# A transformer block on one core: the FFN's down products filled in two halves of columns, each group one product later

## The chip, the cores and the metric

The kernel runs on one core of a Trainium2 chip (trn2). The metric is the device time in microseconds of one execution; three runs of the kernel before give a median of 2186.89 us (2186.75 to 2187.51). The profile is of one more execution, recorded by the hardware profiler.

## What is computed

One decoder block on x of shape (1, 512, 2048) in float32: an RMS norm, one input projection that feeds two groups of attention heads, an output projection, then a SwiGLU FFN with 5632 hidden units, and a final RMS norm. The change touches the FFN alone, which the reference computes so (cut):

```python
hn2 = rmsnorm(h, norm2_g[l])
h = h + (jax.nn.silu(hn2 @ w_gate[l]) * (hn2 @ w_up[l])) @ w_down[l]
return rmsnorm(h, final_g)
```

`w_gate` and `w_up` are 2048 x 5632, `w_down` is 5632 x 2048.

## The kernel before

Everything is kept transposed: channels on the 128 partitions, the 512 tokens as columns. A float32 product is made of three matmuls on split operands (high and low parts in the type fp32r): high weights x high activations, high weights x low activations, low weights x high activations. `mm3` (line 164) and `mm` (line 1009) issue such a trio. Each matmul has a weight load of 128 x 128 ahead of it.

**Halves.** Weights stream in as tiles of 128 x 512, four blocks of 128 x 128. A `Job` (line 123) turns one such tile into a high part on ACT (`first`, line 136, written `wh`) and a low part on DVE (`second`, line 139, written `wl`). Five buffers each rotate. `next_half` (line 172) takes the next job for TensorE, makes sure that the splits run three halves ahead (line 175), and then runs the deferred work in `lag` that has come due; `later(n, f)` (line 183) defers `f` until the half that is n after the next one is about to be issued. In `wsplit` (line 119) the weights lie 32 floats into their buffer where a job has `even=True`, else 16 floats; the streamed operands `ah` and `al` lie 32 floats in. All jobs ahead of the FFN have `even=True`; in the FFN only the first half of P1 for f in (1, 2) or f % 8 == 5 has (line 795).

**Gate and up.** For each of 44 blocks f of 128 hidden units, gate and up are computed together by a scheme of seven products, P1 to P7, in place of eight, on two halves of 256 tokens and 1024 channels. Each product is two halves of 12 matmuls with 256 columns (`product`, line 997). The order for f > 0 is P1, P7, P4, P6, P5, P2, P3. DVE makes the weight sums that the scheme needs (`comb`, line 753) and the sums of products (`after`, line 1027). `finish` (line 1014) then makes silu(gate) x up, splits it, and writes it into block 12 + f % 4 of `ah` (ACT, line 1021) and `al` (DVE, line 1025). For f the chain from the last product P3 to the written `al` is deferred into the products of f + 1: it ends at the half after P7.

**Down.** After four blocks f the four blocks 12 to 15 hold 512 hidden units, and 16 down products (`down`, line 1063) add their share to the 16 blocks of `hs`, the result in SBUF. One down is one half: a tile of `w_down`, 4 blocks x 3 matmuls with 512 columns, into one full bank of PSUM. Two banks rotate in the first group of downs (ph 0), three later. The bank is added to `hs` by DVE (lines 1076 and 1077), due two halves on; in the first group DVE also scales `hs` first. The tiles come by DMA from SP into two buffers (`rawd`, `load_dn`, line 732): each is requested when the one two before it has been split. Gate/up weights come into `raw` (four buffers, `load_to`, line 102), through the same queue.

The downs of one group are set among the seven products of the next f with f % 4 == 0 (f = 4, 8, ..., 40: ten groups, 160 downs), in the list that lines 810 to 823 write out. The last 16 downs are made in the last stage (`last`, line 1103), in halves of 256 tokens, the first half of all 16 outputs ahead of the second, with weights held in tiles that the FFN has finished with.

Of the kernel before, what the change touches and what calls it, by code (L numbers as in the profile page):

```python
# [23 lines left out]
PH = 4  # L24
# [47 lines left out]
def block_kernel(ctx: ExitStack, tc: tile.TileContext, xt, wst, wdn, smalls, wg, w2c, bias, ident_in, out):  # L72
# [17 lines left out]
    ah = slot["h"][:, MH:MH + KB * S].rearrange("p (a b) -> p a b", b=S)  # L90
    al = slot["l"][:, ML:ML + KB * S].rearrange("p (a b) -> p a b", b=S)
# [72 lines left out]
    def mm3(o, wh, wl, mh, ml, start, stop):  # L164
        pe.matmul(o, wh, mh, start=start, stop=False)  # L165
        pe.matmul(o, wh, ml, start=False, stop=False)  # L166
        pe.matmul(o, wl, mh, start=False, stop=stop)  # L167
# [4 lines left out]
    def next_half():  # L172
        i = pos["half"]
        pos["half"] += 1
        split_to(i + (AHEAD[i] if i < len(AHEAD) else 3 if i < len(jobs) - KB - 1 else 4))
        if i < n_plain:
            load_to(i // 2 + LA)
        while lag and lag[0][0] <= i:
            lag.popleft()[1]()
        j = jobs[i]  # L180
        return j.h, j.l

    def later(n, f):
        i = len(lag)
        while i and lag[i - 1][0] > pos["half"] + n:
            i -= 1
        lag.insert(i, (pos["half"] + n, f))
# [464 lines left out]
    def proj_block(upto=None):  # L652
        return ps.tile([128, 512], F32, tag="proj", name="pp", bufs=2)
# [40 lines left out]
    for j in range(NH):  # L694
# [5 lines left out]
        p = proj_block()  # L700
# [8 lines left out]
        p = proj_block()  # L709
# [3 lines left out]
        p = proj_block()  # L713
# [5 lines left out]
        p = proj_block()  # L719
# [81 lines left out]
    def dn_job(p, nb):  # L801
        return Job(lambda: dn[p, nb], post=load_dn)
# [8 lines left out]
    for f in range(FB):  # L811
        qj = quad_jobs(f, ORDER if f else ORDER0)
        p = f // PH - 1
        nb = 0
        for i, name in enumerate(ORDER if f else ORDER0):
            sched.append(("q", f, name))
            jobs += qj[2 * i:2 * i + 2]
            if f and f % PH == 0 and i:
                for _ in range(3 if i < 5 else 4):
                    if nb < KB:  # L820
                        sched.append(("d", p, nb))
                        jobs.append(dn_job(p, nb))
                        nb += 1
# [6 lines left out]
    def out_unit(half, tag="proj"):  # L830
        p = ps.tile([128, 512], F32, tag=tag, name="pab", bufs=2)
        c = 8 - 8 * half
        run_unit([(p, ah[:, c + k, :], al[:, c + k, :], k == 0, k == 7) for k in range(8)])
        return p
# [54 lines left out]
    for nb in range(KB):  # L889
        while "hs" not in rest and (nb == 4 and not idle() or nb == 2 and (queue or cur["s"])):  # L890
            step()
        p = out_unit(1, ("proj", "sc", "t")[nb // 2 % 3])
# [13 lines left out]
    LO, HI = slice(0, 256), slice(256, 512)  # L906
# [72 lines left out]
    for i in range(KB):  # L979
        nb = PASS2[i]  # L980
        p = out_unit(0)
# [27 lines left out]
    def mm(o, wh, wl, mh, ml, start, stop):  # L1009
        pe.matmul(o, wh, mh, start=start, stop=False, skip_group_check=True)  # L1010
        pe.matmul(o, wh, ml, start=False, stop=False, skip_group_check=True)  # L1011
        pe.matmul(o, wl, mh, start=False, stop=stop, skip_group_check=True)  # L1012
# [50 lines left out]
    def down(ph, nb):  # L1063
        n = nb % (3 if ph else 2)
        if n not in dbanks:
            dbanks[n] = banks["P3"] if not n else (ps.tile([128, 512], F32, tag="t", name="pd", bufs=2) if n == 1 else
                                                ps.tile([128, 512], F32, tag="misc", name="pd"))
        p = dbanks[n]
        h, l = next_half()
        for i in range(PH):  # L1070
            mm3(p, h[:, 128 * i:128 * i + 128], l[:, 128 * i:128 * i + 128], ah[:, 12 + i, :], al[:, 12 + i, :],
                i == 0, i == PH - 1)

        def add():
            if not ph:
                dve.tensor_tensor(hs[:, nb, :], hs[:, nb, :], st["inv"], op=OP.mult)
            dve.tensor_tensor(hs[:, nb, :], hs[:, nb, :], p, op=OP.add)  # L1077

        later(1, add)

    for kind, a, b in sched:
        if kind == "d":
            down(a, b)
            continue
        f, name = a, b
        product(f, name)
        if f == 0:
            if name == "P7":
                r = st["rs2"] = Rsqrt(tokens(sacc), D, rab.v[:, :4])
                r.invert()  # L1090
                dve.tensor_tensor(r.z, r.z, rab.y[:, :4], op=OP.mult)
                later(1, lambda r=r: st.update(inv=Spread(r.z), r2=Spread(r.y)))
            if name == "P6":
                st["inv"] = st["inv"](False)
                act.activation(st["rs2"].rs[:, 7, :1], ones[:, :1], AF.Silu)
                st["r2"] = st["r2"](tag="t", bufs=2)
                st["u"] = ft()
            if name in ("P1", "P6", "P3"):
                later(0 if name == "P1" else 1, lambda name=name: after(0, name))
        elif name in ("P1", "P6", "P5", "P2", "P3"):  # L1100
            later({(FB - 1, "P2"): 0, (FB - 1, "P3"): 3}.get((f, name), 1), lambda f=f, name=name: after(f, name))
# [149 lines left out]
```

## Time and profile before

| | |
|---|---|
| median of three runs | 2186.89 us |
| the profiled execution's own time | 2186.78 us |
| its span, first to last instruction | 2185.0 us |
| granted TensorE clock | 0.998 |
| ACT, share of the span | 44% |
| DVE, share of the span | 72% |
| DMA queues, share of 16 engines, the largest | 32.0% |

In the profile PE is TensorE's matmuls and PEld its weight loads, which overlap them; DVE is VectorE, ACT is ScalarE, SP issues DMAs. A group's row gives line, engine, operation, out<-in by the program's names with shapes, the count, then busy time and the mean duration in ns, then idle time before. A row of the timeline gives the start in us from the span's start, the duration, and then the instruction, with idle time ahead of it and what ended it in brackets. A row of the list of waits gives the waiter, what it waited for, and the sum, number and longest in us. The bank that `P3` owns serves as a down's first bank, so that downs appear under the names `P` and `pd`; they are the rows with 512 columns at lines 165 to 167. The last stage's products are named `pl`, those of the output projection `pab`.

### The profile page before, as it was taken

How to read it: one execution, taken by the hardware profiler on the slowest of the kernel's cores; microseconds unless marked ns; L12 is line 12 of the kernel's file. 1: busy time of each engine (PE TensorE's matmuls, PEld its weight loads, DVE VectorE, ACT ScalarE, POOL GpSimd, SP SyncE). 2: the span in 40 equal slices, each digit the busy share in tenths (PEclk: the TensorE clock that was granted, in tenths of full speed). 3: DMA queues.
4: the chain of work that ended last, by engine and by line, in shares of the span. 5: the costliest groups of instructions: out<-in, count | busy, mean ns of one | idle time of the engine just before them, and what ended most of it. 6: DMA issues, size and time to landing. Idle time of an engine off the chain costs nothing.

```text
span 2185.0 us, 35905 instructions
## 1 busy us (share of the span) xinstructions
PE 2166.4 (99%) x13856; PEld 1947.5 (89%) x13856; DVE 1568.1 (72%) x3046; ACT 969.4 (44%) x1862; POOL 43.7 (2%) x51
## 2 busy tenths in 40 slices
PE   9999999999999999999999999999999999999997
PEld 7788888888887889989899999989898999999897
DVE  6755656356667578979687777869596877778686
ACT  6544444344444255535343443435353434434356
POOL 0000000000000000000000000000000000000003
PEclk9999999999999999999999999999999999999999
DMA  6442222322224224332333333323333332333233
GB/s 223 145 138 80 80 80 68 102 87 80 68 89 154 97 97 105 121 111 97 107 107 111 92 116 106 103 93 121 111 97 107 107 112 93 116 106 103 84 125 107
DMA packets 81852, 232.04 MB, mean 106 GB/s; under 512 B 8848, under 2 KB 11536, under 8 KB 81680
## 3 DMA queue, kind: packets, MB, share of 16 engines
q1 hardware_dynamic: 80960, 228.17, 32.0%
q0 software_dynamic: 720, 1.57, 0.5%
q8 instruction: 109, 1.79, 0.3%
q14 instruction: 63, 0.52, 0.1%
HBM read 225.51 MB, written 4.19 MB: 105 GB/s over the span
## 4 chain that ended last, share of the span: by engine, by line
PE 96%; DVE 2%; ACT 1%; issue 0%; DMA 0%; SPq 0%; DVEq 0%; ACTq 0%
PE P L1010 13%; PE P L1012 13%; PE P L1011 13%; PE pp L165 6%; PE pp L167 6%; PE pp L166 6%; PE pd L167 4%; PE pd L166 4%; PE pd L165 4%; PE P L167 3%; PE P L166 3%; PE pab L166 3%; PE pab L167 3%; PE pab L165 3%; PE P L165 3%; PE pt L515 1%
## 5 line engine op out<-in xcount | busy, mean ns | idle before, releaser
L136 ACT ACTIVATE wh<-raw 128x512 fp32r<-128x512 f32 x888 | 548.5, 628 | 514.8 <-PE P L1011 174.0
L139 DVE TENSOR_TENSOR wl<-raw,wh 128x512 fp32r<-128x512 f32 x888 | 596.5, 685 | 61.8 <-ACT wh L136 61.3
L1012 PE MATMUL P<-ah,wl 128*128 128x256 f32 x1056 | 291.8, 276 | 0.3 <-DVE wl L139 0.3
L1010 PE MATMUL P<-ah,wh 128*128 128x256 f32 x1056 | 291.7, 276 | 0.0
L1011 PE MATMUL P<-al,wh 128*128 128x256 f32 x1056 | 291.7, 276 | 0.0
L165 PE MATMUL pp<-ah,wh 128*128 128x512 f32 x640 | 260.4, 407 | 0.0
L167 PE MATMUL pp<-ah,wl 128*128 128x512 f32 x640 | 250.9, 392 | 0.0
L166 PE MATMUL pp<-al,wh 128*128 128x512 f32 x640 | 250.2, 391 | 0.0
L754 DVE TENSOR_TENSOR raw<-raw 128x512 f32<-128x512 f32 x346 | 237.3, 686 | 3.4
L136 ACT ACTIVATE wh<-rawd 128x512 fp32r<-128x512 f32 x160 | 101.1, 632 | 280.5 <-PE pd L166 164.7
L1011 PEld LDWEIGHTS P<-al,wh 128*128 128x128 f32 x1056 | 198.2, 188 | 0.9
L1010 PEld LDWEIGHTS P<-ah,wh 128*128 128x128 f32 x1056 | 198.2, 188 | 0.8
L1012 PEld LDWEIGHTS P<-ah,wl 128*128 128x128 f32 x1056 | 198.2, 188 | 0.5 <-DVE wl L139 0.5
L1077 DVE TENSOR_TENSOR hs<-hs,pd 128x512 f32<-128x512 f32 x98 | 67.4, 687 | 131.5 <-PE pd L167 131.3
L167 PE MATMUL pd<-ah,wl 128*128 128x512 f32 x392 | 154.5, 394 | 0.0
L166 PE MATMUL pd<-al,wh 128*128 128x512 f32 x392 | 153.7, 392 | 0.0
L165 PE MATMUL pd<-ah,wh 128*128 128x512 f32 x392 | 152.1, 388 | 0.0
L167 PEld LDWEIGHTS pp<-ah,wl 128*128 128x128 f32 x640 | 120.2, 188 | 27.9
L165 PEld LDWEIGHTS pp<-ah,wh 128*128 128x128 f32 x640 | 120.5, 188 | 19.6
L166 PEld LDWEIGHTS pp<-al,wh 128*128 128x128 f32 x640 | 120.6, 188 | 19.4
L139 DVE TENSOR_TENSOR wl<-rawd,wh 128x512 fp32r<-128x512 f32 x160 | 109.7, 686 | 23.9 <-ACT wh L136 23.3
L504 ACT ACTIVATE e<-e,st 128x512 f32<-128x512 f32 (+1 forms) x96 | 54.1, 564 | 135.3 <-DVE st L502 135.3
(281 smaller groups left out, 4920.6 us busy)
## 6 DMA issues: line engine op xcount, KB each, us to landing
raw<-in_wst_dram SPq DMA_DIRECT2D x310, 512.0 KB, 3.5
rawd<-in_wdn_dram SPq DMA_DIRECT2D x160, 256.0 KB, 2.6
bias<-in_bias_dram SPq DMA_DIRECT2D x16, 320.0 KB, 2.9
xc<-in_xt_dram SPq DMA_DIRECT2D x16, 256.0 KB, 2.7
hs<-in_xt_dram SPq DMA_DIRECT2D x16, 256.0 KB, 5.1
fin<-in_wdn_dram SPq DMA_DIRECT2D x8, 512.0 KB, 3.6
out_dram<-hs SPq DMA_DIRECT2D x8, 256.0 KB, 2.2
out_dram<-scaled SPq DMA_DIRECT2D x3, 512.0 KB, 2.8
```

Source lines behind the costliest of these rows:

```text
L136: act.activation(self.h, self.src(), AF.Copy)
L139: dve.tensor_tensor(self.l, self.src(), self.h.bitcast(F32), op=OP.subtract)
L165: pe.matmul(o, wh, mh, start=start, stop=False)
L166: pe.matmul(o, wh, ml, start=False, stop=False)
L167: pe.matmul(o, wl, mh, start=False, stop=stop)
L504: act.activation(et, et, AF.Exp, bias=m, scale=-1.0, accum_out=den)
L515: pe.transpose(p[:, 128 * (o + b):128 * (o + b) + 128], self.e[t][:, 128 * b:128 * b + 128], ident)
L754: return lambda: dve.tensor_tensor(o(), o(), x(), op=OP.add)
L1010: pe.matmul(o, wh, mh, start=start, stop=False, skip_group_check=True)
L1011: pe.matmul(o, wh, ml, start=False, stop=False, skip_group_check=True)
L1012: pe.matmul(o, wl, mh, start=False, stop=stop, skip_group_check=True)
L1077: dve.tensor_tensor(hs[:, nb, :], hs[:, nb, :], p, op=OP.add)
```

## The change

Two edits. A down product no longer runs 4 blocks x 3 matmuls over 512 columns, but first 4 x 3 over columns 0 to 255 and then 4 x 3 over columns 256 to 511 of the same bank (`LO` and `HI`, line 906); the accumulation over the first half ends before that over the second begins. And the list places the downs of a group otherwise: none after P7, four each after P4, P6, P5 and P2. Before, they were three after P7, P4, P6 and P5, and four after P2.

```diff
         for i, name in enumerate(ORDER if f else ORDER0):
             sched.append(("q", f, name))
             jobs += qj[2 * i:2 * i + 2]
-            if f and f % PH == 0 and i:
-                for _ in range(3 if i < 5 else 4):
+            if f and f % PH == 0 and i > 1:
+                for _ in range(4):
                     if nb < KB:
                         sched.append(("d", p, nb))
                         jobs.append(dn_job(p, nb))
...
         p = dbanks[n]
         h, l = next_half()
-        for i in range(PH):
-            mm3(p, h[:, 128 * i:128 * i + 128], l[:, 128 * i:128 * i + 128], ah[:, 12 + i, :], al[:, 12 + i, :],
-                i == 0, i == PH - 1)
+        for c in (LO, HI):
+            for i in range(PH):
+                mm(p[:, c], h[:, 128 * i:128 * i + 128], l[:, 128 * i:128 * i + 128], ah[:, 12 + i, c],
+                   al[:, 12 + i, c], i == 0, i == PH - 1)
```

## The prediction

> **What bounds the kernel now.** I read the page's busy times first, then the list of who waited for whom on TensorE, then the groups of instructions with their shapes kept apart, and last the order of time around the down products.
>
> ```profile
> span 2185.0 us, 35905 instructions
> ...
> PE 2166.4 (99%) x13856; PEld 1947.5 (89%) x13856; DVE 1568.1 (72%) x3046; ACT 969.4 (44%) x1862; POOL 43.7 (2%) x51
> ```
> ```profile
> PE P L1012 <- DVE wl L139: 0.3, 1, 0.3
> PE P L1010 <- DVE ft L1047: 0.3, 1, 0.3
> ```
> TensorE is busy for 99% of the span. Of its waits these two stand at the FFN's gate/up products, and none in the list stands at a down product: there is no stall at the downs that the change could take away. What can change is how many matmuls run and how far apart they start. A matmul's own duration in the profile overlaps the next one's, so all my prices are differences of starts.
>
> ```profile
> 1069.53 0.28 PE L1010 MATMUL P<-ah,wh 128*128 128x256 f32 x1
> ...
> 1072.25 0.39 PE L165 MATMUL P<-ah,wh 128*128 128x512 f32 x1
> ...
> 1080.49 0.28 PE L1010 MATMUL P<-T1h,wh 128*128 128x256 f32 x1
> ```
> Here stand, in order, the 24 matmuls of one gate/up product (P6, 256 columns wide), three down products of 12 matmuls with 512 columns each, and the next product's first. The product took 1072.25 - 1069.53 = 2.72 us, 113.3 ns a matmul. The three downs took 1080.49 - 1072.25 = 8.24 us, 2.747 us each, 228.9 ns a matmul. Two matmuls of 256 columns thus take 226.7 ns, 2.2 ns less than one of 512 here, for the same columns. That is the point of the whole argument: the wide matmuls of the downs are the slower way to stream these columns.
>
> They are not slow for their width alone:
>
> ```profile
> 838.01 0.39 PE L165 MATMUL pab<-ah,wh 128*128 128x512 f32 x1
> ...
> 840.73 0.39 PE L165 MATMUL pab<-ah,wh 128*128 128x512 f32 x1
> ```
> Twelve 512-wide matmuls of the output projection took 2.72 us. Those weights are laid at another offset (`even=True`, 32 floats in) than the downs' (16 floats in). So the 0.027 us excess of a down depends on how weights and streamed columns lie, and it has to be shown that 256-wide downs are free of it.
>
> **The change part by part.**
>
> *The split.* A down of 12 matmuls x 512 columns becomes 24 x 256: the same columns, the same weights, each weight slice loaded twice as often.
>
> ```profile
> L167 PE MATMUL pd<-ah,wl 128*128 128x512 f32 x392 | 154.5, 394 | 0.0
> ...
> L167 PE MATMUL P<-ah,wl 128*128 128x512 f32 x248 | 97.7, 394 | 0.0
> ```
> (392 + 248) / 4 = 160 downs go through the changed function, all but the last 16, which the last stage already does in halves. That last stage is therefore the nearest row for the new price. It streams the same four blocks of `ah` and `al` (12 to 15), first columns 0 to 255 for all 16 outputs, then 256 to 511:
>
> ```profile
> 2126.17 0.28 PE L165 MATMUL pl<-ah 128*128 128x256 f32 x1
> ...
> 2153.37 0.30 PE L211 MATMUL prs<-ones,sacc 128*128 128x32 f32 x2
> ```
> Between these starts lie 16 outputs of the first half and 4 of the second, 240 matmuls in 27.20 us: 113.3 ns each, for both halves of the columns, at the products' own pace. Its weights lie 16 floats in, as the downs' do. The P6 row above adds the other thing needed: weights out of the rotating buffers with columns of `ah`/`al`, also at 113.3. So a split down costs 24 x 113.3 ns = 2.720 us against 2.747, and 160 of them save 160 x 0.0267 = **4.27 us**. The bounds of this price: 2.72 below, since no row of 256-wide matmuls is quicker; 2.747 above, if the downs keep their excess whatever their width (no gain). A third row, a slower pace of 256-wide matmuls, is left to the first rival, because it needs an event that starts it. I take 2.72, the price of the rows that share the operands.
>
> The Trainium skill speaks against the split: "TensorE: Matmul & The Clock Gate", section Back-to-back issue gap, gives a gap of the column count over 2.4 GHz plus about 2.5 ns for each matmul. By that the 1920 added matmuls would cost an estimated 4.8 us and the time would be 2191.7. The rows above do not have such a fixed part: 113.3 doubled is 226.7, just the 2.72 us / 12 of the output projection.
>
> *The move.* Each group of downs starts after P4 in place of P7, and its pieces are 4, 4, 4, 4 in place of 3, 3, 3, 3, 4. No instruction is added. What it does to the waits is seen in the group that starts at 1050.33:
>
> ```profile
> 1050.26 0.63 ACT L136 ACTIVATE wh<-rawd 128x512 fp32r<-128x512 f32 x1 [3.10 <-DMA rawd<-in_wdn_dram]
> 1050.80 0.62 ACT L1021 ACTIVATE ah<-ft 128x512 fp32r<-128x512 f32 x1
> ```
> ```profile
> 1051.54 0.68 DVE L1025 SCALAR_TENSOR_TENSOR al<-ft,ah 128x512 fp32r<-128x512 f32 x1
> ```
> ```profile
> 1050.33 0.39 PE L165 MATMUL P<-ah,wh 128*128 128x512 f32 x1
> ...
> 1052.62 0.39 PE L166 MATMUL P<-al,wh 128*128 128x512 f32 x1
> ```
> ACT waits 3.10 us for the third down's weights, and the last activation block (L1021, then `al` on DVE) is queued behind that wait. `al` is ready at 1052.22; TensorE wants it in the fourth block at 1052.62, 0.40 us later. With halves and no move that matmul would come 10 x 0.113 = 1.13 us after the group's start, at 1051.46: 0.76 us of stall in each of 10 groups, 7.6 us, more than the split saves. With the move the same matmul comes 2.72 + 1.13 us after 1050.33, at 1054.18, some 2 us after `al`; and L1021 is now issued ahead of the wait for the third down, not behind it. The move costs nothing, covered by P4 on TensorE, and buys the split its cover.
>
> The DMA side of the move:
>
> ```profile
> raw<-in_wst_dram SPq DMA_DIRECT2D x310, 512.0 KB, 3.5
> rawd<-in_wdn_dram SPq DMA_DIRECT2D x160, 256.0 KB, 2.6
> ```
> The number of transfers stays. SP's queue is in order, and the next block's `raw` requests (after P6 and P5) come two downs and one down earlier in it. Two `rawd` buffers give one down per half of (2.6 landing + 0.63 on ACT + 0.69 on DVE) = 2.0 us, against 2.72 us of TensorE; a `raw` of 3.5 us between them is a single delay, and a down's weights are split three halves ahead. In the first group, with two banks, the sum into `hs` must end before the next-but-one down:
>
> ```profile
> 934.33 0.69 DVE L1077 TENSOR_TENSOR hs<-hs,P 128x512 f32<-128x512 f32 x1
> ...
> 935.64 0.39 PE L165 MATMUL P<-ah,wh 128*128 128x512 f32 x1
> ```
> It ends at 935.02, 0.6 us ahead. In the new order five DVE operations stand between the third down's `wl` and that sum (six now), so about the same is left; if it is lost, TensorE waits once, and the first rival says what that costs.
>
> Sum: 2186.78 (the profiled execution: span 2185.0 and 1.8 around it) - 4.27 = 2182.5. The median of the runs, 2186.89, lies 0.11 higher, so the forecast is **2182.6 us**.
>
> **The rivals.**
>
> *A. A wait throws TensorE into a slower pace.* Some 256-wide matmuls run slower, and the trace shows when:
>
> ```profile
> 875.38 0.39 PE L1012 MATMUL P<-ah,wl 128*128 128x256 f32 x1 [0.30 <-DVE wl L139]
> ...
> 876.31 0.28 PE L1010 MATMUL P<-ah,wh 128*128 128x256 f32 x1
> ...
> 877.73 0.28 PE L1010 MATMUL P<-ah,wh 128*128 128x256 f32 x1
> ...
> 987.69 0.28 PE L1010 MATMUL P<-B11h,wh 128*128 128x256 f32 x1
> ...
> 989.13 0.28 PE L1010 MATMUL P<-B11h,wh 128*128 128x256 f32 x1
> ```
> After a wait of some tenths of a microsecond, 12 matmuls take 1.42 us in place of 1.36, and the pace comes back only with a half whose weights lie at the other offset (line 795: f = 1, 2 and f = 5, 13, ...; such a half takes 1.44 us, the last two rows). The product of f = 8 and the last stage, above, are at 1.36 a half. With the downs in 256 columns, a wait in a group would slow all that follows until the next such half. If every group had one: 160 downs at 2.84 instead of 2.747 are +15 us. Slow products: from the group of f = 8 to the half in f = 13 they are 4 + 21 + 7 = 32, four such pairs make 128, f = 4 adds 4, and f = 40 to 43 add 4 + 21; 157 at 0.12 us are +19 us. Ten waits near 0.6 us (875.38 came 0.58 late) are +6 us: 2227 us. It decides from one wait per group on. For it: the price is in the trace. Against: the margins above grow or stay. If only the two-bank group is hit, 14 downs and 4 products at 0.12 us and a wait of 0.3, 2.5 us, are given back: 2185.1. The skill's page on TensorE (section LDWEIGHTS) puts a load of 128 columns at an estimated 128/1.2 = 107 ns, as long as 256 columns stream; the cadence of 113.3 agrees that nothing is left over.
>
> *B. Each matmul has a start cost.* If the downs' 2.2 ns over the projection's 226.7 belong to starting a matmul, halves pay it twice: +4.3 us, 2191.1. Against: the last stage's 240 matmuls show none. The skill's rule cited above is of this kind.
>
> *C. The excess follows the downs, not the width.* Then 24 x 114.4 = 2.747 and the time stays at 2186.9. Against: the last stage streams the same blocks without it; for: it uses its weights from resident tiles.
>
> **How the numbers follow.** Forecast 0.80, A in every group 0.08, A in the two-bank group 0.03, B 0.04, C 0.05. About 0.2% (4.37 us) is what a measurement of this kernel can tell from no change: below 2182.52 is faster, above 2191.26 slower. The forecast lies 0.1 us on the near side of the lower bound. What the sum leaves out leans down: the five later `even` halves cost 1.44 - 1.36 = 0.08 us each, 0.4 us, and may cost less when nothing 512 wide runs ahead of them. I split the 0.80 into 0.50 faster and 0.30 within. Faster 0.50; same 0.30 + 0.03 + 0.05 + half of B = 0.40; slower 0.08 + 0.02 = 0.10. The range goes from 2181.9 (the sum less 0.4 and 0.3 of the runs' spread) to 2187.2 (C and its spread), leaving out A in every group and B. The forecast alone: 2181.9 to 2183.1.
>
> **What would show it.** Right: down matmuls of 256 columns at 113.3 ns, 2.72 us a down, products still 1.36 a half, no wait at a down, `al` ready some 2 us early. Wrong: starts 117 to 118 ns apart after a group (A), 114.4 in the downs alone (C) or more (B), or a wait by TensorE for `hs`, `al` or `wl` within a group.

## The result, and the profile after

The changed kernel takes 2182.66 us, median of 20 runs (2181.97 to 2186.92), against 2187.59 us for the kernel before in 20 runs beside it (2186.75 to 2197.23): ratio 0.9978, 95% interval [0.9972, 0.9984]. The forecast was 2182.6 us. The ratios here and below leave out runs more than 1.5% above the fastest of their kernel; where a kernel has such runs, its whole range is given.

From the page of the changed kernel:

```profile
span 2180.6 us, 39719 instructions
...
PE 2161.7 (99%) x15776; PEld 2021.7 (93%) x15776; DVE 1568.4 (72%) x3046; ACT 970.5 (45%) x1862; POOL 43.7 (2%) x51
```
TensorE has 15776 - 13856 = 1920 matmuls more, and as many loads, in a span 4.4 us shorter. The timeline of TensorE in the group of f = 8, from its first down to the product behind the fourth:

```profile
1052.48 0.28 PE L1010 MATMUL P<-ah,wh 128*128 128x256 f32 x1
...
1063.37 0.28 PE L1010 MATMUL P<-ah,wh 128*128 128x256 f32 x1
```
Four downs in 10.89 us are 2.72 us each (2.747 before), 113.4 ns a matmul. All ten groups are like it: 43.52 us for 16 downs, where they were 43.95. That is 4.27 us of the 4.4; the rest is of this one execution alone (in f = 1 the products went on at 1.36 a half behind their wait, 0.4 us less, and the first stage had one more wait of 0.3). The wait in f = 1, and two matmuls a half apart behind it:

```profile
875.64 0.39 PE L1012 MATMUL P<-ah,wl 128*128 128x256 f32 x1 [0.29 <-DVE wl L139]
875.87 0.28 PE L1010 MATMUL P<-ah,wh 128*128 128x256 f32 x1
...
877.23 0.28 PE L1010 MATMUL P<-ah,wh 128*128 128x256 f32 x1
```
The like wait in the kernel before was followed by halves of 1.42 us (the first rival's rows).

What the move did, for the same group, DVE and TensorE in one timeline:

```profile
1049.22 0.69 DVE L1025 SCALAR_TENSOR_TENSOR al<-ft,ah 128x512 fp32r<-128x512 f32 x1
...
1053.62 0.28 PE L1011 MATMUL P<-al,wh 128*128 128x256 f32 x1
```
`al` is done at 1049.91, the matmul that needs it in the fourth block starts at 1053.62: 3.7 us of cover, where 0.40 us were; it is 3.7 us in all ten groups. And the two-bank group (f = 4), the sum into `hs` and the down that takes its bank again:

```profile
936.92 0.69 DVE L1078 TENSOR_TENSOR hs<-hs,P 128x512 f32<-128x512 f32 x1
...
938.16 0.28 PE L1010 MATMUL P<-ah,wh 128*128 128x256 f32 x1
```
It ends at 937.61, 0.55 us ahead (0.6 before). The end of TensorE's list of waits names no down, as before:

```profile
PE P L1010 <- DVE ft L1047: 0.3, 1, 0.3
PE P L1012 <- DVE wl L139: 0.3, 1, 0.3
PE pc L166 <- DVE al L255: 0.3, 1, 0.3
```

### The profile page after: what moved, and what is told of

Its sections match the earlier page's. It is cut to its first block, busy times and chain, and to the rows that moved or that the text cites. A ratio compares the mean times of both kernels' runs of the same rounds, so it can differ in the third digit from the quotient of the medians.

```text
span 2180.6 us, 39719 instructions
## 1 busy us (share of the span) xinstructions
PE 2161.7 (99%) x15776; PEld 2021.7 (93%) x15776; DVE 1568.4 (72%) x3046; ACT 970.5 (45%) x1862; POOL 43.7 (2%) x51
## 4 chain that ended last, share of the span: by engine, by line
PE 96%; DVE 2%; ACT 1%; issue 0%; DMA 0%; SPq 0%; DVEq 0%; ACTq 0%
PE P L1012 15%; PE P L1010 15%; PE P L1011 15%; PE pp L165 6%; PE pp L167 6%; PE pp L166 6%; PE pd L1011 4%; PE pd L1010 4%; PE pd L1012 4%; PE pab L166 3%; PE pab L167 3%; PE pab L165 3%; PE pt L515 1%; PE psc L167 1%; PE psc L166 1%; PE psc L165 1%
## 5 line engine op out<-in xcount | busy, mean ns | idle before, releaser
L1012 PE MATMUL P<-ah,wl 128*128 128x256 f32 x1552 | 428.9, 276 | 0.3 <-DVE wl L139 0.3
L1010 PE MATMUL P<-ah,wh 128*128 128x256 f32 x1552 | 428.8, 276 | 0.0
L1011 PE MATMUL P<-al,wh 128*128 128x256 f32 x1552 | 428.8, 276 | 0.0
L1012 PEld LDWEIGHTS P<-ah,wl 128*128 128x128 f32 x1552 | 291.4, 188 | 0.5 <-DVE wl L139 0.5
L1010 PE MATMUL pd<-ah,wh 128*128 128x256 f32 x784 | 216.6, 276 | 0.0
L1012 PE MATMUL pd<-ah,wl 128*128 128x256 f32 x784 | 216.6, 276 | 0.0
L1011 PE MATMUL pd<-al,wh 128*128 128x256 f32 x784 | 216.5, 276 | 0.0
L1011 PEld LDWEIGHTS pd<-al,wh 128*128 128x128 f32 x784 | 147.2, 188 | 0.0
L1010 PEld LDWEIGHTS pd<-ah,wh 128*128 128x128 f32 x784 | 147.2, 188 | 0.0
L1012 PEld LDWEIGHTS pd<-ah,wl 128*128 128x128 f32 x784 | 147.2, 188 | 0.0
```

## The experiments

Below, "quick" is 1.360 us for a half of 12 matmuls with 256 columns, "slow" 1.413; an even half is one whose weights lie 32 floats into their buffer.

### 1. The split without the move

The downs stay where they were; the edit is against the kernel before.

```diff
-        for i in range(PH):
-            mm3(p, ..., ah[:, 12 + i, :], al[:, 12 + i, :], i == 0, i == PH - 1)
+        for c in (LO, HI):
+            for i in range(PH):
+                mm(p[:, c], ..., ah[:, 12 + i, c], al[:, 12 + i, c], i == 0, i == PH - 1)
```

> Halves, but the downs stay after P7, P4, P6, P5 and P2 as before. Theory (al is late, and a wait starts the slower pace): TensorE waits about 0.76 us for al in each of the 10 groups (7.6 us), then 12 matmuls of 256 columns take 1.41 us until a half with even=True: downs at 2.83 us, +13 us over before, some 163 slow products at 0.107 us (+17 us) and the last stage (+1 us): about 2226 us. Rival 1 (a wait costs itself alone): 2186.9 - 4.3 + 7.6 = 2190 us, downs at 2.72. Rival 2 (al comes in time after all, the move is idle): 2182.6 us, no waits at L1011.

Three runs: 2217.47, 2202.47 and 2192.89 us, ratio 1.0068 [1.0028, 1.0109]. TensorE and DVE in the profiled one (2217.47), group of f = 8:

```profile
1052.66 0.68 DVE L1025 SCALAR_TENSOR_TENSOR al<-ft,ah 128x512 fp32r<-128x512 f32 x1
...
1053.40 0.39 PE L1011 MATMUL P<-al,wh 128*128 128x256 f32 x1 [0.34 <-DVE al L1025]
...
1055.15 0.28 PE L1010 MATMUL pd<-ah,wh 128*128 128x256 f32 x1
```
TensorE waits for `al`: 1053.40 should have been 1052.89, half a microsecond. The 14 matmuls to the next down take 1.75 us; past the first, of 0.22, they are 117 to 118 ns apart, and stay so through f = 9 to 20: products of 2.83, downs of 2.83. This is the mechanism that was expected, but not its extent. Of ten groups only this one shows a wait. In f = 4 a delay too small for the list is enough:

```profile
930.78 0.28 PE L1010 MATMUL P<-ah,wh 128*128 128x256 f32 x1
930.90 0.33 PE L1011 MATMUL P<-al,wh 128*128 128x256 f32 x1
931.06 0.28 PE L1012 MATMUL P<-ah,wl 128*128 128x256 f32 x1
```
The step from 930.90 to 931.06 is 0.16 us in place of 0.11; everything behind it is slow until f = 5. In f = 24 it was less:

```profile
1548.60 0.31 PE L1011 MATMUL P<-al,wh 128*128 128x256 f32 x1
1548.74 0.28 PE L1012 MATMUL P<-ah,wl 128*128 128x256 f32 x1
```
Here 0.14 us in place of 0.11, and the pace is slow until f = 37: 178 halves x 0.053 and 64 downs x 0.107, an estimated 16 us for 0.03 us of delay. In f = 40, `al` came 0.27 us ahead and the group stayed quick. The other six groups were already in the slow pace when they began. So of the four groups that began quick, three were made slow. That the two other runs differ from this one by which groups were hit is likely, but they were not profiled; none of the three came under 2192.

### 2. The move without the split

The edit is against the changed kernel.

```diff
-        for c in (LO, HI):
-            for i in range(PH):
-                mm(p[:, c], ..., ah[:, 12 + i, c], al[:, 12 + i, c], i == 0, i == PH - 1)
+        for i in range(PH):
+            mm3(p, ..., ah[:, 12 + i, :], al[:, 12 + i, :], i == 0, i == PH - 1)
```

> The downs are moved but keep 512 columns. Theory (the gain is all the split's; the move is cover): 2186.9 us, 0.0 us from before, downs at 2.747 us each. Rival (the move gives part of the gain by itself): up to 4.3 us faster, with downs still at 2.747 and time saved at waits.

2187.82 us, median of 12 (2186.91 to 2189.31); ratio 0.9997 [0.9986, 1.0007]. Four downs of f = 8, from the first to the product behind them:

```profile
1053.16 0.39 PE L165 MATMUL P<-ah,wh 128*128 128x512 f32 x1
...
1064.15 0.28 PE L1010 MATMUL P<-ah,wh 128*128 128x256 f32 x1
```
10.99 / 4 = 2.747 us a down, and the products are quick. The move by itself is worth nothing that can be measured; the gain is the split's, and the first run shows that the split without it loses.

### 3. No even half in the FFN

```diff
-        r["P1", 0].even = f in (1, 2) or f % 8 == 5
+        r["P1", 0].even = False
```

> The changed kernel with no half at the other weight offset (line 795 gives False for all f). Theory (the slower pace lasts until such a half): the pace of f = 0 (1.413 us a half) stays to the end of the FFN: 588 halves of f = 2 to 43 at +0.053 (31.4 us), 160 downs at 2.827 in place of 2.720 (17.1 us), f = 1 and the last stage (+1.4 us), less 0.6 us for the even halves themselves: about 2232 us. Rival (the pace recovers by itself after some time, even halves only cost): 2182.1 us, halves at 1.360 from some point on.

2231.80 and 2232.51 us; ratio 1.0195 [1.0163, 1.0227]. Four downs of f = 8, as above:

```profile
1059.94 0.28 PE L1010 MATMUL P<-ah,wh 128*128 128x256 f32 x1
...
1071.24 0.28 PE L1010 MATMUL P<-ah,wh 128*128 128x256 f32 x1
```
11.30 / 4 = 2.83 us a down; halves without a wait take 1.413 from f = 0 to the last stage. The slow pace does not end by itself in 1.3 ms.

### 4 and 5. The other offset, for wide downs and for halves

The fourth run is the kernel before, the fifth the changed kernel, each with

```diff
-        return Job(lambda: dn[p, nb], post=load_dn)
+        return Job(lambda: dn[p, nb], post=load_dn, even=True)
```

> The kernel before, order and 512 columns kept, with the downs' weights 32 floats into their buffers (even=True) as in the output projection. Theory (a wide down's excess comes from the weights' offset, and the pace of the products after wide matmuls depends on it as well): downs at 2.720 us (-4.3 us), but the products behind them at 1.413 us a half, as those of f = 0 behind the output projection, until the next even half: some 163 products at +0.107 us (+17.4 us) and the last stage +1.1: about 2201 us. Rival 1 (the offset changes the downs alone): 2182.6 us, as good as the split. Rival 2 (the excess belongs to the downs whatever the offset): 2186.9 us, downs at 2.747.

2201.97 us, median of 5 (2201.09 to 2202.02); ratio 1.0058 [1.0039, 1.0077]. Two downs and the product behind them, in f = 8:

```profile
1052.94 0.39 PE L165 MATMUL pd<-ah,wh 128*128 128x512 f32 x1
...
1055.66 0.39 PE L165 MATMUL pd<-ah,wh 128*128 128x512 f32 x1
...
1058.38 0.28 PE L1010 MATMUL P<-T4h,wh 128*128 128x256 f32 x1
...
1061.21 0.40 PE L165 MATMUL P<-ah,wh 128*128 128x512 f32 x1
```
A wide down costs 2.72 with this offset, so its excess was the offset's; but the product behind it takes 2.83, slow. The first down of each piece takes 2.73 behind slow products and 2.75 or 2.76 behind quick ones, so the 160 downs save 3.7 us, not 4.3, and this is paid back about fivefold by some 17 us at the products and 1.1 in the last stage.

> The changed kernel with the downs' weights 32 floats into their buffers (even=True). Theory (the price of 256 columns depends on the offset): 12 matmuls take 1.44 us as in the even halves of f = 5, 13, ...: 160 downs at 2.88 in place of 2.72 us, +25.6 us: about 2208 us, the products still at 1.36 a half. Rival (with 256 columns the offset does not matter): 2182.7 us.

2207.93 and 2209.57 us; ratio 1.0099 [1.008, 1.0117]. Four downs of f = 8, and no product between them:

```profile
1056.61 0.28 PE L1010 MATMUL P<-ah,wh 128*128 128x256 f32 x1
...
1068.12 0.28 PE L1010 MATMUL P<-ah,wh 128*128 128x256 f32 x1
```
11.51 / 4 = 2.88 us a down. Of the four ways to lay and cut a down, only halves at 16 floats are cheap and leave the products quick.

### 6. The kernel before with no even half

The same line as in the third run, in the kernel before.

> The kernel before with no even half in the FFN (line 795 gives False). Theory (a wide down ends the slower pace, so that the kernel before was guarded by its downs): slow from f = 0 to the first downs of f = 4, 38 halves at 0.053 (+2.0 us) less 0.6 us for the even halves: 2188.4 us, halves at 1.360 from f = 4 on. Rival (wide downs leave the pace as it is): all products slow, +32 us and more: about 2219 us.

Ten runs: four from 2185.92 to 2188.67, six from 2218.68 to 2220.60. Three downs and the next product of f = 8, in a run of 2219.62:

```profile
1055.25 0.39 PE L165 MATMUL P<-ah,wh 128*128 128x512 f32 x1
...
1063.49 0.28 PE L1010 MATMUL P<-T4h,wh 128*128 128x256 f32 x1
...
1066.32 0.39 PE L165 MATMUL P<-ah,wh 128*128 128x512 f32 x1
```
My theory falls: a wide down does not end the slow pace. It takes 8.24 / 3 = 2.747 us in the slow pace as in the quick one, and the product behind it is slow again, 2.83. The rival's 2219 is the time of six runs. By their times the other four were quick without any even half, so it seems that the pace can also become quick by chance; none of the four was profiled.

### 7. Even halves for f = 1 and 2 alone

The changed kernel with `f in (1, 2)` in line 795.

> The changed kernel with even halves for f = 1 and 2 alone (those of f = 5, 13, 21, 29 and 37 taken out). Theory (no wait from f = 3 on, so nothing is left for these halves to mend): 5 x 0.08 = 0.4 us faster than the change, about 2182.3 us, all halves from f = 3 on at 1.360. Rival (something slows the pace in some group and these halves mend it): products at 1.413 a half from some f on, up to 30 us slower.

2182.28 us, median of 10 (2182.01 to 2182.90); ratio 0.9978 [0.9969, 0.9987]. All halves and downs from f = 3 on are quick: no group starts the slow pace by itself. In these ten runs f = 2 always mended, which is not assured: the eighth run has the same even halves, and there it missed.

### 8 and 9. One matmul more

Into the changed kernel with even halves for f = 1 and 2 alone (8), and into the changed kernel itself (9):

```diff
         product(f, name)
+        if (f, name) == (9, "P4"):
+            pe.matmul(dbanks[2][:, :32], ones, ones[:, :32], start=True, stop=True)
```

> The changed kernel with even halves for f = 1 and 2 alone (as in the seventh run), and one more matmul of 32 columns, into a bank that nobody reads then, behind P4 of f = 9. Theory (any break of the even run of loads and streams starts the slower pace, which lasts until something mends it): 484 halves of f = 9 to 43 at +0.053 (25.8 us), 128 downs at +0.107 (13.7 us), the last stage +1.1: 40.6 us over 2182.3, about 2223 us, from one matmul. Rival (the matmul costs itself): 2182.4 us.

Four runs: 2222.60, 2222.84, 2231.53 and 2232.56 us; ratio 1.0176 [1.0159, 1.0194]. The first two are the expected 2223: 40 us from one small matmul, by their times. The profiled one, 2232.56, was slow from the wait in f = 1 on, before the added matmul: the even half of f = 2 took 1.443 us and the pace stayed slow. That the matmul itself sets the slow pace is therefore seen in the trace of the ninth run alone.

> The changed kernel itself, even halves of f = 5, 13, 21, 29 and 37 kept, with the same one matmul behind P4 of f = 9. Theory (the even half of f = 13 ends the slower pace): 50 halves at +0.053 (2.7 us) and 16 downs at +0.107 (1.7 us) over 2182.7: about 2187.1 us; if the half of f = 13 misses, as two of five did in the run with the split alone, it lasts to f = 21: 112 + 50 halves and 48 downs, +13.8 us, 2196 us. Rival (even halves do not end it): as without them, about 2223 us. Rival (the matmul costs itself): 2182.8 us.

2196.34 us, median of 4 (2195.84 to 2196.78); ratio 1.0042 [1.0029, 1.0056]: the case in which f = 13 misses, in all four runs by their times. The inserted matmul in f = 9 (TensorE), which leaves two records (x2):

```profile
1115.14 0.30 PE L1089 MATMUL pd<-ones 128*128 128x32 f32 x2
1115.28 0.37 PE L1010 MATMUL P<-ah,wh 128*128 128x256 f32 x1
1115.49 0.28 PE L1011 MATMUL P<-al,wh 128*128 128x256 f32 x1
```
and the even halves of f = 13 and f = 21, each with the half and the product behind it:

```profile
1231.26 0.28 PE L1010 MATMUL P<-B11h,wh 128*128 128x256 f32 x1
...
1232.70 0.28 PE L1010 MATMUL P<-B11h,wh 128*128 128x256 f32 x1
...
1234.12 0.28 PE L1010 MATMUL P<-ah,wh 128*128 128x256 f32 x1
```
```profile
1480.03 0.28 PE L1010 MATMUL P<-B11h,wh 128*128 128x256 f32 x1
...
1481.46 0.28 PE L1010 MATMUL P<-B11h,wh 128*128 128x256 f32 x1
...
1482.82 0.28 PE L1010 MATMUL P<-ah,wh 128*128 128x256 f32 x1
```
f = 13: 1.44, then 1.42, still slow. f = 21: 1.43, then 1.36, quick. So the halves of f = 5, 13, 21, 29 and 37, which cost 0.4 us, are a guard, but one that can miss. In this trace all but the even halves are quick from f = 2 to the inserted matmul, and slow from behind it to f = 21.

### 10. Even halves where the slow pace starts

Even halves for f = 0, 1 and 2 alone, and in the last stage the weights of output 7 at 32 floats.

```diff
-        r["P1", 0].even = f in (1, 2) or f % 8 == 5
+        r["P1", 0].even = f < 3
...
-            return tuple(slot[t + x][:, at + 512 * n:at + 512 * n + 512] for x, at in (("h", WH), ("l", WL)))
+            return tuple(slot[t + x][:, at + 512 * n:at + 512 * n + 512] for x, at in ((("h", MH), ("l", ML)) if nb == 7 else (("h", WH), ("l", WL))))
```

> The changed kernel with even halves for f = 0, 1 and 2 alone, and the weights of the last stage's output 7 laid 32 floats in. Theory: 0.4 us for the five later halves, 0.3 us for the products of f = 0 that then run at 1.360 in place of 1.413, and 0.3 us in the last stage (outputs 8 to 15 of the second half of columns at 1.36 in place of 1.413, output 7 at 1.44 in the first): about 2181.7 us. Rival (these places do not mend the pace): 2182.4 us.

Eleven runs: nine from 2181.20 to 2183.38, two at 2230.17 and 2230.53; ratio of the nine 0.9975 [0.9966, 0.9985]. The profiled run is one of the two: the even half of f = 0 took 1.434 us and mended, but f = 2 missed (1.442), and from the wait in f = 1 on all was slow until output 7, behind which the rest was quick in both halves of the columns. So these places can mend. The gain is not shown: the nine runs' median is 2182.25 us, nearer to the rival's 2182.4 than to the expected 2181.7.

### 11 and 12. Two even halves in a row

The changed kernel with `f in (1, 2, 3)` (11), and the tenth kernel with `f < 4` (12).

> The changed kernel with even halves for f = 1, 2 and 3 alone. What the runs so far show: an even half that misses (1.442 us, the pace stays slow) was followed by one that mends (1.430) each time there was a next one, whereas no product from f = 3 on starts the slow pace by itself. Theory (two even halves in a row are a sure cure, so f = 3 replaces the five later ones): 2182.7 - 5 x 0.08 + 0.08 = about 2182.3 us in most runs, and at most 2183.2 where f = 2 misses (14 halves at 0.053), with no run at 2186 or 2230. Rival (a miss is independent of the one before): now and then a run near 2228 us, as with f = 1 and 2 alone it could be.

2182.35 us, median of 11 (2181.91 to 2183.22); ratio 0.9979 [0.997, 0.9987].

> Even halves for f = 0, 1, 2 and 3 alone, and the last stage's output 7 with its weights 32 floats in, as in the tenth run, which had profiled runs of its products of f = 0 and of its last outputs at 1.360 and one run in five near 2230. Theory: 2182.3 less 0.3 (f = 0) less 0.3 (last stage): about 2181.7 us, and no run near 2230, since f = 3 mends what f = 2 misses. Rival (f = 3 misses too in some runs): runs near 2229 us again.

2181.74 us, median of 10 (2181.45 to 2182.63); ratio 0.9976 [0.9967, 0.9986]. No run of either kernel was near 2186 or 2230. In the profiled run of each, f = 2 mended, so that a cure by f = 3 was not seen at work; in that of the twelfth, output 7 missed in the second half of columns, and its last outputs were slow. The twelfth kernel is the fastest of all by its median, 0.9 us below the changed one, though their intervals against the kernel before overlap, and the kernel before had 2187.09 us beside the twelfth and 2187.59 beside the changed one.

## Why the prediction was right, step by step

- **No wait at the downs to take away.** Right; the second run, without any time for the move alone, shows it.
- **The split: 160 x (2.747 - 2.720) = 4.27 us.** Right to 0.01 us by the traces: the 160 downs took 439.46 us and take 435.20. That the median came within 0.06 us of the forecast is partly luck. The kernel before had 2187.59 us beside the changed one, 0.70 more than the base of the forecast, so the medians differ by 4.93 us, not 4.27. Nothing in a trace accounts for the other 0.66; the kernel before had medians from 2186.97 to 2187.36 beside the experiments. The last stage was the proper row: same blocks, same offset, both halves of the columns. That the excess of a wide down hangs on the offset was an inference from the output projection, and the fourth run shows it.
- **No start cost per matmul (rival B).** Right: 24 matmuls take 2.72 us, the time of 12 wide ones at their best. The rule of 2.5 ns a matmul in the Trainium skill ("TensorE: Matmul & The Clock Gate", Back-to-back issue gap) would have made an estimated 1920 x 2.5 = 4.8 us; these matmuls do not show it. The section calls this the gap of an isolated matmul and gives other figures for a stream of loads and matmuls, which the prediction did not say; none of them is for 256 columns.
- **The excess stays with the downs (rival C).** Refuted by the same rows.
- **The move is cover.** Right in kind, and larger than said: 3.7 us, not 2, since `al` itself came earlier as well, no longer behind ACT's wait for the third down's weights.
- **The split alone stalls 0.76 us in each of 10 groups.** This step was wrong. It took the group of f = 8 for all ten, and that was the worst. In f = 12 of the kernel before:

```profile
1170.44 0.39 PE L165 MATMUL P<-ah,wh 128*128 128x512 f32 x1
...
1170.65 0.68 DVE L1025 SCALAR_TENSOR_TENSOR al<-ft,ah 128x512 fp32r<-128x512 f32 x1
```
`al` is ready at 1171.33, 0.89 us after the group's first down, not 1.89, and 0.24 ahead of a matmul at 1.13. The nine groups other than f = 8 lie between 0.76 and 1.15. So there were not ten stalls of 0.76: the first run had one wait of half a microsecond, two delays of 0.05 and 0.03 us where `al` came only some 0.1 us ahead (f = 4 and 24), and lost up to 30 us by the pace instead.
- **Rival A, "after a wait of some tenths of a microsecond" the pace is slow.** Right as a mechanism; its price was a little high, with 1.42 us a half and 2.84 a down for 1.413 and 2.827. With these two the third run's 2232 and the eighth's 2223 came as worked out. Wrong in three points: a single delay of 0.03 us can be enough to decide, where it asked for one wait per group, a wait does not always set the slow pace (in f = 1 of the changed kernel it did not), and an even half does not always bring the quick pace back. It did not happen in the groups of the changed kernel, where no down has a delay: every down and product from f = 3 on is quick in its profile.
- **The even halves "may cost less".** No: 1.440 us, 0.08 each, as before.

Open: two of the 20 runs of the changed kernel took 2186.3 and 2186.9. A miss at f = 2 that f = 5 mends would cost 42 halves x 0.053 + 16 downs x 0.107 = 3.9 us, which fits; no such run was profiled. What decides between mending and missing was not found either. One sign of it is in the traces, read in ns: where the pace was slow, the step from the last matmul ahead into the even half (f = 2 and later) is 115 ns in all 17 that mend and 117 or 118 ns in all 6 that miss, so it is settled by the even half's first matmul. In the first, fifth and ninth runs each miss was followed by an even half that mended, which is why the last two kernels have two in a row. And why the offset changes the time of a matmul, one way at 512 columns and the other at 256, stays open.

## What to carry to other kernels

Price a matmul by the distance between starts, with its operands' offsets and its width as they will be, from a row that has all of them. A bound engine that runs without a gap can have two paces, as TensorE has here, and a single late operand can cost hundreds of times its own delay (an estimated 16 us for 0.03 in the first run); when a change tightens the cadence, move the nearly late operand's consumer back first. One group's margin is not the margin of all groups: look at each before multiplying.

## What the runs showed of the hardware that was not expected

- Time of one down (the same multiply-adds), by width and offset of the weights: 512 columns at 16 floats 2.747 us, in either pace; 512 at 32 floats 2.72 (the first of a piece 2.73 to 2.76), with slow products behind it; 256 at 16 floats 2.720 quick and 2.827 slow; 256 at 32 floats 2.88, with quick products behind it.
- The pace of 256-wide matmuls, 113.3 or 117.8 ns apart, is a state that persists: one matmul of 32 columns set it to slow until an even half mended it 365 us later (ninth run), and with no even half behind it cost 40 us (eighth run, by the times). Rows of TensorE's waits do not show it, since no matmul waits; only the distance between starts does. A weight load of 128 columns is put at an estimated 128 / 1.2 = 107 ns by the Trainium skill ("TensorE: Matmul & The Clock Gate", LDWEIGHTS), nearly what 256 columns take here. No run here shows a load's time by itself (its rows give 188 ns, but overlap as the matmuls' do), and that two streams of nearly equal length make the pace sensitive is a guess.
- An even half in the slow pace of the FFN takes 1.430 us and mends, or 1.442 to 1.443 us and does not; in the quick pace it takes 1.440.
